# Hybrid encoder block on one core: moving the matmul operands to byte addresses that are multiples of 256 or 2048

## The chip, the cores and the metric

The kernel runs on one core of a Trainium2 chip. The metric is the device time of one execution in microseconds (us); lower is better.

## The reference

One layer of a hybrid sequence encoder, batch 1, 512 tokens, width 1024, all in float32. Cut to what matters here:

```
h = rms_norm(x, norm1_g)
p = h @ w_in                                  # 1024 -> 11520 columns: the "projections"
y_a = b_a * causal_dwconv(c_a * x_a)          # short gated convolution
y_b = rg_lru(causal_dwconv(x_b)) * gelu(g_b)  # linear recurrence over the tokens
y_c = rwkv7(token_shift(p_c)) * g_c           # matrix-state recurrence, 16 heads, chunks of 64
m = gate_a*y_a + gate_b*y_b + gate_c*y_c
x = x + m @ w_out                             # 1024 -> 1024
x = x + square(relu(rms_norm(x) @ mlp_w1)) @ mlp_w2   # 1024 -> 4096 -> 1024
return rms_norm(x, final_g)
```

## The kernel before

**Dense products.** Every dense float32 product is made of three matmuls. Each operand is split into a high part (the value rounded to the matmul's input type) and a low part (what is left), and `mm3` (lines 155 to 158) issues high times high, high times low, low times high, all into one PSUM tile. In each of them one operand is stationary (loaded into the array first, 128 x 128) and the other is streamed through it (128 x 512, or 128 x 256 where half the tokens are done).

**Weights.** `load_w` fetches 128 rows of weights in two halves of 128 x 512. `load_half` (lines 130 to 137) issues the DMA from the SP queue into `raw`, ScalarE casts it to the high part `whi` (L134), and VectorE subtracts to get the low part `wlo` (the helper `tt`, L97). There are three buffers for `raw` and four each for `whi` and `wlo`; all lie next to each other in the memory of each partition. 340 halves go through these buffers in all.

**Stages**, in order of time (us from the start of the span):

- 0 to 30: the tokens' norm; weights begin to load.
- 30 to 747: projections. 90 chunks of 128 output columns. For 87 of them `proj` (from L271) streams the normed input `hh`, `hl` (eight slices of 512 tokens each) against the weights, so the weight is stationary: 24 matmuls a chunk, into PSUM tile `pp`. Three first chunks use the unscaled input `xgh`, `xgl` instead. Between them stand the small matmuls of the recurrence (`pA`, `pu`, `py`, `pS`, ...) and small dense products (`pga`, `pgi` with the weights `swbh`, `swbl` and the streamed operand `uh`, `ul`).
- 747 to 770: `w_out`, eight chunks for each half of the tokens, 24 matmuls of 256 columns each, streaming `mh`, `ml`; PSUM tile `acc`. (The first half's matmuls lie partly before 747.)
- 770 to 953: first MLP product, 32 chunks (`fi`), streaming `h2h`, `h2l` against weights; PSUM tile `p1`, which the profile calls `p`. The first chunk is done in two halves of 256 columns. ScalarE and VectorE make the squared ReLU of each chunk and its parts `ah`, `al` (`ah2`, `al2` from chunk 24 on).
- 953 to 1130: second MLP product. Here the roles are swapped: slices of `ah`, `al` are stationary, and the weights `whi`, `wlo` are streamed, into eight PSUM tiles `acc`; 32 x 24 matmuls.
- 1130 to 1137: the last norm and the output.

**What sets the order.** The kernel is written in a tile language. Its scheduler fixes one order of instructions for each engine, from the order of the code and the priorities in it (`OFF`, `CP`, `R0` and others). Places in memory come from pools: a tile of a pool that grows from the left follows the tile before it, one of a pool on the right (`htp`, `pro`, `wk`, `h2p`, `xrp`) is counted down from the end of the partition. No address is written by hand; the default alignment is 32 bytes.

Of the kernel before, what the change touches and what calls it, by code (L numbers as in the profile page):

```python
# [10 lines left out]
F32R = mybir.dt.float32r  # L11
# [7 lines left out]
P = 128  # L19
# [8 lines left out]
NWARM = 2  # L28
POOL_KT = (1, 3, 5, 6, 7)
S = 512  # L30
D = 1024
KT = 8
NG = 4
# [3 lines left out]
NF = FF // P  # L37
# [54 lines left out]
def block_kernel(ctx, tc, xt, win, par, mulr, sw, wout, w1, w2, fg, cst, eyes, out):  # L92
# [18 lines left out]
    wp = ctx.enter_context(tc.tile_pool(name="wp", bufs=2))  # L111
# [18 lines left out]
    def load_half(src, i):  # L130
        raw = wp.tile([P, S], F32, tag="raw", name="raw", bufs=3)
        sy.dma_start(raw, src[:, i * S:(i + 1) * S])
        hi = wp.tile([P, S], F32R, tag="whi", name="whi", bufs=4)
        ac.copy(hi, raw)  # L134
        lo = wp.tile([P, S], F32R, tag="wlo", name="wlo", bufs=4)
        tt(lo, raw, f(hi), SUB)
        return hi, lo

# [8 lines left out]
    def split(pool, src, tag, rows=slice(0, P), bufs=None):  # L147
        th, tl = tag if type(tag) is tuple else (tag + "h", tag + "l")
        hi = pool.tile([P, S], F32R, tag=th, name=th, bufs=bufs)
        lo = pool.tile([P, S], F32R, tag=tl, name=tl, bufs=bufs)  # L150
        ac.copy(hi[rows], src)
# [36 lines left out]

    ht_ctx = ExitStack()
    htp = ht_ctx.enter_context(tc.tile_pool(name="htp", bufs=1, side="right"))  # L190
    hh = htp.tile([P, KT, S], F32R, name="hh")
    hl = htp.tile([P, KT, S], F32R, name="hl")

    ps = ExitStack()
    pp = ps.enter_context(tc.tile_pool(name="pp", bufs=3, space=PSUM))
# [3 lines left out]
    pro = pro_ctx.enter_context(tc.tile_pool(name="pro", bufs=1, side="right"))  # L199
# [2 lines left out]
    xT = sp.tile([P, KT, S], F32, tag="AXt", name="xT")  # L202
    xgh_ = [sp.tile([P, 4, S], F32R, tag=t, name="xgh") for t in ("BKT", "Z")]
    xgh = lambda kt: xgh_[kt // 4][:, kt % 4]
    xgl = pro.tile([P, KT, S], F32R, name="xgl")
    rsb = pro.tile([P, S], F32, name="rsb")
    ones = pro.tile([P, P], F32, name="ones")
    zer = sp.tile([P, S], F32, tag="dg", name="zer")
# [439 lines left out]
    M = {"done": []}  # L648
# [152 lines left out]
    def open_m():  # L801
        pk_ctx.close()
        mo = mo_ctx.enter_context(tc.tile_pool(name="mo", bufs=1))
        mh = M["mh"] = mo.tile([P, KT, S], F32R, name="mh")
        ml = M["ml"] = mo.tile([P, KT, S], F32R, name="ml")
        mab = M["mab"] = mo.tile([P, 2, S], F32, name="mab")
        for q in M["done"]:
            gp.dma_start(mh[:, q], mhd[q])
            gp.dma_start(ml[:, q], mld[q])
        gp.dma_start(mab, mpd[6:8].rearrange("q p t -> p q t"))  # L810
        M["mo"] = mo
        return
        yield

    def last_fill():
        yield from fill_main(NG - 1)
        M["gts"] = []
        for h in range(2):
            q = 6 + h
            gt = yield from gate_c(sp, q, f"bv{h}")  # L820
            g2_mul(wk, q, gt)
            M["gts"].append(gt)
            yield
        wk_ctx.close()
        ht_ctx.close()
        h2p = h2_ctx.enter_context(tc.tile_pool(name="h2p", bufs=1, side="right"))
        M["h2h"] = h2p.tile([P, KT, S], F32R, name="h2h")
        M["h2l"] = h2p.tile([P, KT, S], F32R, name="h2l")
        xrp = xr_ctx.enter_context(tc.tile_pool(name="xrp", bufs=1, side="right"))
        M["xrp"] = xrp  # L830
        x2T = M["x2T"] = xrp.tile([P, KT, S], F32, name="x2T")
        for i in range(4):
            gp.dma_start(x2T[:, 2 * i:2 * i + 2], xt[2 * i:2 * i + 2].rearrange("k p t -> p k t"))
        while "half" not in M:
            yield
        fin_m(0)
        yield from w_out(0)
# [53 lines left out]
    h2h, h2l = M["h2h"], M["h2l"]  # L891
# [6 lines left out]
    NA = 3 * NF // 4  # L898
    with tc.tile_pool(name="mw", bufs=2) as mw, \
            tc.tile_pool(name="ap", bufs=1) as apool, \  # L900
            ExitStack() as apool2:
        ahs = [apool.tile([P, NA, S], F32R, name="ah")]
        als = [apool.tile([P, NA, S], F32R, name="al")]
        ahl = lambda fi: (ahs[fi // NA][:, fi % NA], als[fi // NA][:, fi % NA])

        def mlp1(t, w, tl):
            for kt in range(KT):
                wh, wl = wslice(w, kt)
                mm3(t[:, tl], wh, wl, h2h[:, kt, tl], h2l[:, kt, tl],
                    start=kt == 0, stop=kt == KT - 1)  # L910

        for fi in range(NF):
            t = pp.tile([P, S], F32, tag="pp", name="p1")
            w = load_w(w1[fi])
            if fi == 0:
                for th in range(2):
                    mlp1(t, w, slice(th * HT, (th + 1) * HT))
            else:
                mlp1(t, w, slice(0, S))
            if fi == 0:  # L920
                drain(to_tokens(1))
            r = mw.tile([P, S], F32, tag="r", name="r")
            ac.activation(r, t, AF.Relu)
            tt(r, r, r, MUL)
            if fi == NA:
                xr_ctx.close()
                ap2 = apool2.enter_context(tc.tile_pool(name="ap2", bufs=1))
                ahs.append(ap2.tile([P, NF - NA, S], F32R, name="ah2"))
                als.append(ap2.tile([P, NF - NA, S], F32R, name="al2"))
            ahi, alo = ahl(fi)  # L930
            ac.copy(ahi, r)
            tt(alo, r, f(ahi), SUB)
        ac.activation(epst, epst, AF.Sqrt)
        gp.memset(epst, EPS)

        sc2 = cp.tile([P, 4], F32, name="sc2")
        tt(sc2, ss2[:, 0], ss2[:, 1], ADD)
        ts2(sc2, sc2, 1.0 / D, EPS, MUL, ADD)
        v.reciprocal(sc2, sc2)
        h2_ctx.close()  # L940
        with tc.tile_pool(name="fin", bufs=1, side="right") as fin:
            xr = fin.tile([P, 4, D], F32, name="xr2")
            gp.dma_start(xr, x2d.rearrange("i p d -> p i d"))
            fgt = fin.tile([P, D], F32, name="fgt")
            gp.dma_start(fgt, fg.to_broadcast([P, D]))
            bank = lambda pool, tag: pool.tile([P, S], F32, tag=tag, name="acc")
            acc = [[bank(pc, "pu"), bank(pc, "pS")], [bank(pc, "py"), bank(pm, "pm")],
                   [bank(pm, "pm"), bank(pp, "pp")], [bank(pp, "pp"), bank(pp, "pp")]]

            def mlp2(fi, w, i, h):  # L950
                ms = slice(i * P, (i + 1) * P)
                ahi, alo = ahl(fi)
                mm3(acc[i][h], ahi[:, ms], alo[:, ms], w[h][0], w[h][1],
                    start=fi == 0, stop=fi == NF - 1)

            for fi in range(NF - 2):
                w = load_w(w2[fi])
                for i in range(4):
                    for h in range(2):
                        mlp2(fi, w, i, h)  # L960
            wl2 = [load_w(w2[fi]) for fi in range(NF - 2, NF)]
            def last(i):
                ss = fin.tile([P, 2], F32, tag="fss", name="fss", bufs=2)
                x3f = xr[:, i] if i < 3 else fin.tile([P, D], F32, name="x3f")
                for h in range(2):
                    hs = slice(h * S, (h + 1) * S)
                    for d_ in range(2):
                        mlp2(NF - 2 + d_, wl2[d_], i, h)
                    stt(xr[:, i, hs], acc[i][h], sc2[:, i:i + 1], xr[:, i, hs], MUL, ADD)
                    junk = fin.tile([P, S], F32, tag="fj", name="fj", bufs=2)  # L970
                    ac.activation(junk, xr[:, i, hs], AF.Square, accum_out=ss[:, h:h + 1])
                    (v if (i, h) == (3, 0) else gp).tensor_tensor(out=x3f[:, hs], in0=xr[:, i, hs], in1=fgt[:, hs], op=MUL)
                sd = fin.tile([P, 2], F32, tag="fsd", name="fsd", bufs=2)
                tt(sd[:, 0:1], ss[:, 0:1], ss[:, 1:2], ADD)
                ac.activation(sd[:, 1:2], sd[:, 0:1], AF.Sqrt, bias=epst[:, 0:1], scale=1.0 / D)
                v.reciprocal(sd[:, 0:1], sd[:, 1:2])
                yield
                for h in range(2):
                    hs = slice(h * S, (h + 1) * S)
                    if h == 0 and i != 2:  # L980
                        ac.activation(x3f[:, hs], x3f[:, hs], AF.Copy, scale=sd[:, 0:1])
                    else:
                        v.tensor_scalar(out=x3f[:, hs], in0=x3f[:, hs], scalar1=sd[:, 0:1], scalar2=None, op0=MUL)
                    (ac if h == 0 and i != 2 else sy).dma_start(out[i, :, hs], x3f[:, hs])

            gens = [last(i) for i in range(4)]
            for i in (0, 1, 2, 0, 1, 3, 3, 2):
                next(gens[i], None)
        ps.close()
# [74 lines left out]
```

## Time and profile before

| What | Value |
|---|---|
| median of three executions | 1141.97 us (1141.84 to 1142.87) |
| the profiled execution's own time | 1139.16 us |
| its span, first to last instruction | 1137.4 us |
| mean granted TensorE clock | 0.985 of full speed |
| TensorE matmuls (PE) busy | 1102.8 us, 97% of the span |
| VectorE (DVE) busy | 786.2 us, 69% |
| ScalarE (ACT) busy | 549.1 us, 48% |
| mean DMA rate | 101 GB/s |

How to read it: matmuls overlap. One of 512 columns is shown as some 0.39 to 0.41 us long, but the next one starts after some 0.23 us, so the distance from start to start is what a matmul costs in a dense row of them, not its duration.

### The profile page before, as it was taken

How to read it: one execution, taken by the hardware profiler on the slowest of the kernel's cores; microseconds unless marked ns; L12 is line 12 of the kernel's file. 1: busy time of each engine (PE TensorE's matmuls, PEld its weight loads, DVE VectorE, ACT ScalarE, POOL GpSimd, SP SyncE). 2: the span in 40 equal slices, each digit the busy share in tenths (PEclk: the TensorE clock that was granted, in tenths of full speed). 3: DMA queues.
4: the chain of work that ended last, by engine and by line, in shares of the span. 5: the costliest groups of instructions: out<-in, count | busy, mean ns of one | idle time of the engine just before them, and what ended most of it. 6: DMA issues, size and time to landing. Idle time of an engine off the chain costs nothing.

```text
span 1137.4 us, 17256 instructions
## 1 busy us (share of the span) xinstructions
PE 1102.8 (97%) x6396; PEld 867.8 (76%) x6396; DVE 786.2 (69%) x1537; ACT 549.1 (48%) x1005; POOL 58.9 (5%) x99
## 2 busy tenths in 40 slices
PE   8899989999999999999999999999999999999996
PEld 4677877778777778777777667898888888888885
DVE  7998996889976979976979957786444444222225
ACT  6655456534557534557534565565444443222224
POOL 3200000000000000000000020100000000000003
PEclk8899999999999999999999999999999999999998
DMA  5222222222332222332221262554322225322232
GB/s 190 76 95 63 85 83 71 71 93 68 95 112 76 76 93 68 101 107 75 75 89 65 84 195 75 176 188 160 96 94 94 93 93 178 107 95 93 93 102 93
DMA packets 61973, 114.69 MB, mean 101 GB/s; under 512 B 7232, under 2 KB 10816, under 8 KB 61888
## 3 DMA queue, kind: packets, MB, share of 16 engines
q1 hardware_dynamic: 54960, 95.49, 26.0%
q0 software_dynamic: 6352, 17.30, 4.7%
q8 instruction: 50, 0.82, 0.3%
q10 hardware_dynamic: 576, 0.79, 0.2%
q14 instruction: 35, 0.29, 0.1%
HBM read 104.64 MB, written 8.91 MB: 100 GB/s over the span
## 4 chain that ended last, share of the span: by engine, by line
PE 81%; DVE 14%; issue 3%; ACT 2%; DMA 0%; SPq 0%; DVEq 0%; ACTq 0%
PE pp L158 11%; PE pp L156 11%; PE pp L157 11%; PE acc L157 6%; PE acc L156 6%; PE acc L158 6%; PE p L158 5%; PE p L156 5%; PE p L157 5%; DVE wlo L97 3%; PE pA L461 2%; DVE Z L97 2%; DVE dg L97 2%; PE py L568 1%; DVE g L100 1%
## 5 line engine op out<-in xcount | busy, mean ns | idle before, releaser
L97 DVE TENSOR_TENSOR wlo<-raw,whi 128x512 fp32r<-128x512 f32 x340 | 235.8, 696 | 242.0 <-ACT whi L134 232.3
L134 ACT CAST whi<-raw 128x512 fp32r<-128x512 f32 x340 | 209.8, 619 | 364.3 <-PE acc L158 122.7
L158 PE MATMUL pp<-hh,wlo 128*128 128x512 f32 x696 | 284.0, 409 | 14.8 <-DVE wlo L97 14.7
L157 PE MATMUL pp<-hl,whi 128*128 128x512 f32 x696 | 281.5, 404 | 3.1 <-DVE hl L100 3.1
L156 PE MATMUL pp<-hh,whi 128*128 128x512 f32 x696 | 281.9, 406 | 1.3 <-ACT hh L257 1.3
L158 PEld LDWEIGHTS pp<-hh,wlo 128*128 128x128 f32 x696 | 132.6, 191 | 52.7 <-DVE wlo L97 21.7
L157 PEld LDWEIGHTS pp<-hl,whi 128*128 128x128 f32 x696 | 132.5, 190 | 34.1 <-DVE hl L100 3.7
L156 PEld LDWEIGHTS pp<-hh,whi 128*128 128x128 f32 x696 | 132.6, 190 | 32.8 <-ACT hh L257 1.8
L158 PE MATMUL p<-h2h,wlo 128*128 128x512 f32 (+1 forms) x264 | 103.0, 390 | 0.0
L156 PE MATMUL p<-h2h,whi 128*128 128x512 f32 (+1 forms) x264 | 102.9, 390 | 0.0
L157 PE MATMUL p<-h2l,whi 128*128 128x512 f32 (+1 forms) x264 | 102.8, 389 | 0.0
L157 PE MATMUL acc<-wlo,ah 128*128 128x512 f32 x256 | 99.7, 389 | 0.0
L156 PE MATMUL acc<-whi,ah 128*128 128x512 f32 x256 | 99.6, 389 | 0.0
L158 PE MATMUL acc<-whi,al 128*128 128x512 f32 x256 | 99.6, 389 | 0.0
L158 PEld LDWEIGHTS p<-h2h,wlo 128*128 128x128 f32 x264 | 49.7, 188 | 11.4
L157 PEld LDWEIGHTS p<-h2l,whi 128*128 128x128 f32 x264 | 49.7, 188 | 11.3
L156 PEld LDWEIGHTS p<-h2h,whi 128*128 128x128 f32 x264 | 49.7, 188 | 11.2
L157 PEld LDWEIGHTS acc<-wlo,ah 128*128 128x128 f32 x256 | 48.0, 188 | 10.1 <-DVE wlo L97 0.3
L156 PEld LDWEIGHTS acc<-whi,ah 128*128 128x128 f32 x256 | 48.0, 188 | 10.1
L158 PEld LDWEIGHTS acc<-whi,al 128*128 128x128 f32 x256 | 48.1, 188 | 10.0
L97 DVE TENSOR_TENSOR dg<-Z 64x31 f32<-64x31 f32 (+15 forms) x124 | 42.2, 340 | 4.1
L97 DVE TENSOR_TENSOR Z<-Z,dg 64x31 f32<-64x31 f32 (+15 forms) x124 | 42.2, 340 | 4.1
(299 smaller groups left out, 1525.4 us busy)
## 6 DMA issues: line engine op xcount, KB each, us to landing
raw<-in_win SPq DMA_DIRECT2D x180, 256.0 KB, 2.6
raw<-in_w SPq DMA_DIRECT2D x128, 256.0 KB, 2.6
raw<-in_wout SPq DMA_DIRECT2D x32, 256.0 KB, 2.6
swr<-in_sw SPq DMA_DIRECT2D x16, 128.0 KB, 2.2
x2T<-in_xt POOLq DMA_DIRECT2D x4, 512.0 KB, 6.3
x2d<-st POOLq DMA_DIRECT2D x8, 256.0 KB, 3.2
xr<-x2d POOLq DMA_DIRECT2D x1, 2048.0 KB, 8.9
xT<-in_xt SPq DMA_DIRECT2D x3, 512.0 KB, 6.1
```

The source lines that it names most:

```text
L97: return v.tensor_tensor(out=o, in0=a, in1=b, op=op)
L100: return v.scalar_tensor_tensor(out=o, in0=a, scalar=s, in1=b, op0=op0, op1=op1)
L134: ac.copy(hi, raw)
L156: pe.matmul(ps, wh, xh, start=start, stop=False)
L157: pe.matmul(ps, wh, xl, start=False, stop=False)
L158: pe.matmul(ps, wl, xh, start=False, stop=stop)
L461: pe.matmul(pts[h][:, ci], G_.BK[rows, jj, c], G_.AR[rows, jj, c], start=True, stop=True)
L568: mm = pe.matmul(py[64 * h:64 * h + 64, jj], w, x, start=first and jj == 0, stop=last, skip_group_check=True)
```

## The change

Tiles that are operands of the dense matmuls get an alignment: `AL` = 256 bytes, and `ALM` = 2048 bytes for the streamed operand of the first MLP product and the stationary one of the second.

```
+AL, ALM = 256, 2048
     def load_half(src, i):
-        hi = wp.tile([P, S], F32R, tag="whi", name="whi", bufs=4)
+        hi = wp.tile([P, S], F32R, tag="whi", name="whi", bufs=4, align_bytes=AL)
-        lo = wp.tile([P, S], F32R, tag="wlo", name="wlo", bufs=4)
+        lo = wp.tile([P, S], F32R, tag="wlo", name="wlo", bufs=4, align_bytes=AL)
...
+    hh = htp.tile([P, KT, S], F32R, name="hh", align_bytes=AL)
+    hl = htp.tile([P, KT, S], F32R, name="hl", align_bytes=AL)
...
+    xgl = pro.tile([P, KT, S], F32R, name="xgl", align_bytes=AL)
...
+        mh = M["mh"] = mo.tile([P, KT, S], F32R, name="mh", align_bytes=AL)
+        ml = M["ml"] = mo.tile([P, KT, S], F32R, name="ml", align_bytes=AL)
...
+        M["h2h"] = h2p.tile([P, KT, S], F32R, name="h2h", align_bytes=ALM)
+        M["h2l"] = h2p.tile([P, KT, S], F32R, name="h2l", align_bytes=ALM)
...
+        ahs = [apool.tile([P, NA, S], F32R, name="ah", align_bytes=ALM)]
+        als = [apool.tile([P, NA, S], F32R, name="al", align_bytes=ALM)]
...
+                ahs.append(ap2.tile([P, NF - NA, S], F32R, name="ah2", align_bytes=AL))
+                als.append(ap2.tile([P, NF - NA, S], F32R, name="al2", align_bytes=AL))
```

The two built programs hold the same 9,856 instructions, in the same order on each engine and with the same waits. What differs is where tiles lie in each partition. The table gives the byte address of each operand as built, and its remainder by 256 and by 512. All buffers of a tag lie 2048 bytes apart and the 512-byte slices of weights that a matmul loads follow each other, so every stationary slice of `whi` has the remainder of the table too; the same holds for all slices of the others (a half of the tokens is 1024 bytes).

| Tile | before: address, by 256, by 512 | after: address, by 256, by 512 |
|---|---|---|
| `whi` (first buffer) | 25152, 64, 64 | 25344, 0, 256 |
| `wlo` (first buffer) | 33344, 64, 64 | 33792, 0, 0 |
| `hh`, `hl` | 196576 and 212960, 224, 480 | 196352 and 212736, 0, 256 |
| `xgh` | 59968, 64, 64 | 60416, 0, 0 |
| `xgl` | 170720, 224, 224 | 170240, 0, 256 |
| `mh` | 123072, 192, 192 | 123648, 0, 256 |
| `ml` | 139456, 192, 192 | 140288, 0, 0 |
| `h2h`, `h2l` | 196576 and 212960, 224, 480 | 194560 and 210944, 0, 0 |
| `ah`, `al` | 47680 and 96832, 64, 64 | 49152 and 100352, 0, 0 |
| `ah2` | 145984, 64, 64 | 150528, 0, 0 |
| `al2` | 162368, 64, 64 | 167168, 0, 256 |
| `uh`, `ul`, `swbh`, `swbl` (no alignment asked) | 175072, 177120, 185312, 186336: 224, 480 | 174624, 176672, 184864, 185888: 32, 32 |

The other tiles of the recurrence move by a few hundred bytes with their pools.

More of the change, by code (lines that the diff above doesn't have):

```diff
@@ L190, in block_kernel @@
     htp = ht_ctx.enter_context(tc.tile_pool(name="htp", bufs=1, side="right"))
-    hh = htp.tile([P, KT, S], F32R, name="hh")
-    hl = htp.tile([P, KT, S], F32R, name="hl")
+    hh = htp.tile([P, KT, S], F32R, name="hh", align_bytes=AL)
+    hl = htp.tile([P, KT, S], F32R, name="hl", align_bytes=AL)
     ps = ExitStack()
@@ L204, in block_kernel @@
     xgh = lambda kt: xgh_[kt // 4][:, kt % 4]
-    xgl = pro.tile([P, KT, S], F32R, name="xgl")
+    xgl = pro.tile([P, KT, S], F32R, name="xgl", align_bytes=AL)
     rsb = pro.tile([P, S], F32, name="rsb")
@@ L803, in open_m @@
         mo = mo_ctx.enter_context(tc.tile_pool(name="mo", bufs=1))
-        mh = M["mh"] = mo.tile([P, KT, S], F32R, name="mh")
-        ml = M["ml"] = mo.tile([P, KT, S], F32R, name="ml")
+        mh = M["mh"] = mo.tile([P, KT, S], F32R, name="mh", align_bytes=AL)
+        ml = M["ml"] = mo.tile([P, KT, S], F32R, name="ml", align_bytes=AL)
         mab = M["mab"] = mo.tile([P, 2, S], F32, name="mab")
@@ L826, in last_fill @@
         h2p = h2_ctx.enter_context(tc.tile_pool(name="h2p", bufs=1, side="right"))
-        M["h2h"] = h2p.tile([P, KT, S], F32R, name="h2h")
-        M["h2l"] = h2p.tile([P, KT, S], F32R, name="h2l")
+        M["h2h"] = h2p.tile([P, KT, S], F32R, name="h2h", align_bytes=ALM)
+        M["h2l"] = h2p.tile([P, KT, S], F32R, name="h2l", align_bytes=ALM)
         xrp = xr_ctx.enter_context(tc.tile_pool(name="xrp", bufs=1, side="right"))
@@ L901, in block_kernel @@
             ExitStack() as apool2:
-        ahs = [apool.tile([P, NA, S], F32R, name="ah")]
-        als = [apool.tile([P, NA, S], F32R, name="al")]
+        ahs = [apool.tile([P, NA, S], F32R, name="ah", align_bytes=ALM)]
+        als = [apool.tile([P, NA, S], F32R, name="al", align_bytes=ALM)]
         ahl = lambda fi: (ahs[fi // NA][:, fi % NA], als[fi // NA][:, fi % NA])
@@ L927, in block_kernel @@
                 ap2 = apool2.enter_context(tc.tile_pool(name="ap2", bufs=1))
-                ahs.append(ap2.tile([P, NF - NA, S], F32R, name="ah2"))
-                als.append(ap2.tile([P, NF - NA, S], F32R, name="al2"))
+                ahs.append(ap2.tile([P, NF - NA, S], F32R, name="ah2", align_bytes=AL))
+                als.append(ap2.tile([P, NF - NA, S], F32R, name="al2", align_bytes=AL))
             ahi, alo = ahl(fi)
```

## The prediction

> **What bounds the kernel now.** First the page's busy times and its chain of work that ended last:
>
> ```profile
> PE 1102.8 (97%) x6396; PEld 867.8 (76%) x6396; DVE 786.2 (69%) x1537; ACT 549.1 (48%) x1005; POOL 58.9 (5%) x99
> ...
> PE 81%; DVE 14%; issue 3%; ACT 2%; DMA 0%; SPq 0%; DVEq 0%; ACTq 0%
> PE pp L158 11%; PE pp L156 11%; PE pp L157 11%; PE acc L157 6%; PE acc L156 6%; PE acc L158 6%; PE p L158 5%; PE p L156 5%; PE p L157 5%; DVE wlo L97 3%; PE pA L461 2%; DVE Z L97 2%; DVE dg L97 2%; PE py L568 1%; DVE g L100 1%
> ```
>
> TensorE sets the end: 81% of the chain, of which `pp` (projections) 33%, `acc` (mostly the second MLP product) 18% and `p` (the first) 15%. So I ask what one matmul costs. A window inside the projections, one of the first MLP product and one of the second:
>
> ```profile
> 200.00:300.00 100.00, 99.86 (x585) 76.93 (x585) 88.13 (x183) 49.88 (x92) 2.79 (x6) 1.00 0.24 77
> 758.00:768.00 10.00, 10.00 (x87) 10.00 (x86) 8.08 (x16) 6.50 (x14) 0.54 (x1) 1.00 0.60 204
> 800.00:940.00 140.00, 140.00 (x599) 112.54 (x598) 66.48 (x100) 59.00 (x100) 0.00 (x0) 1.00 0.29 94
> 955.00:1035.00 80.00, 80.00 (x355) 66.24 (x354) 20.38 (x30) 18.47 (x30) 0.48 (x1) 1.00 0.38 129
> ```
>
> Columns: window, then busy us and count of PE, weight loads, DVE, ACT, POOL, then granted clock, DMA share, GB/s. In both MLP windows PE never idles and the granted clock is 1.00, the matmuls have the same shape, and yet the first makes 599 in 140 us (234 ns each) and the second 355 in 80 us (225 ns each). A count includes one or two begun before its window, so the exact distance comes from the start times (first column):
>
> ```profile
> 945.05 0.39 PE L156 MATMUL p<-h2h,whi 128*128 128x512 f32 x1
> 945.28 0.40 PE L157 MATMUL p<-h2l,whi 128*128 128x512 f32 x1
> 945.51 0.40 PE L158 MATMUL p<-h2h,wlo 128*128 128x512 f32 x1
> ...
> 948.33 0.39 PE L158 MATMUL p<-h2h,wlo 128*128 128x512 f32 x1
> ```
>
> From 945.05 to 948.33 there are 14 steps: 234.3 ns each. The second product:
>
> ```profile
> 954.84 0.39 PE L156 MATMUL acc<-whi,ah 128*128 128x512 f32 x1
> 955.07 0.39 PE L157 MATMUL acc<-wlo,ah 128*128 128x512 f32 x1
> 955.29 0.39 PE L158 MATMUL acc<-whi,al 128*128 128x512 f32 x1
> ...
> 957.56 0.39 PE L156 MATMUL acc<-whi,ah 128*128 128x512 f32 x1
> ```
>
> Twelve steps in 2.72 us: 226.7 ns. So two rates exist, 7.6 ns apart, at one clock and one shape. What differs is where the operands lie. In the table of addresses, the streamed `h2h` has remainder 224 by 256 and the stationary `whi` 64: unequal. In the second product both sides have 64: equal. A third place tells whether the value or the equality matters:
>
> ```profile
> 92.18 0.40 PE L156 MATMUL pp<-hh,whi 128*128 128x512 f32 x1
> 92.41 0.40 PE L157 MATMUL pp<-hl,whi 128*128 128x512 f32 x1
> ...
> 93.57 0.39 PE L156 MATMUL pgi<-uh,swbh 128*128 128x512 f32 x1
> ...
> 94.25 0.40 PE L156 MATMUL pp<-hh,whi 128*128 128x512 f32 x1
> ```
>
> The three `pgi` matmuls, from 93.57 to 94.25, take 226.7 ns each amid the projections, with DVE and ACT at work. Their operands `uh`, `ul`, `swbh`, `swbl` all have remainder 224: equal again, though not 64. The `pp` row before (224 against 64) takes 230 ns in this piece. So I read: equal remainders give 226.7, unequal ones 234.3. It is a regularity in rows, not a mechanism that they show.
>
> **The change part by part.** It puts `whi`, `wlo` and every dense partner at remainder 0 by 256, so unequal pairs become equal. No instruction, DMA or wait is added, removed or moved; the order on each queue is the same. Only durations can change.
>
> *First MLP product.* 31 chunks x 24 = 744 matmuls, 7.6 ns each: 5.7 us. All of it lands, since PE has no idle time there and DVE is busy 66.48 of 140 us, ACT 59.00: there is room.
>
> *Projections.* 87 chunks x 24 = 2088 matmuls x 7.6 = 15.9 us at most. Not all of it lands:
>
> ```profile
> L158 PE MATMUL pp<-hh,wlo 128*128 128x512 f32 x694 | 282.7, 408 | 14.8 <-DVE wlo L97 14.7
> L156 PE MATMUL pp<-hh,whi 128*128 128x512 f32 x693 | 280.2, 406 | 0.0
> L157 PE MATMUL pp<-hl,whi 128*128 128x512 f32 x694 | 280.1, 404 | 0.0
> L97 DVE TENSOR_TENSOR wlo<-raw,whi 128x512 fp32r<-128x512 f32 x190 | 130.2, 687 | 42.2 <-ACT whi L134 36.9 <-PE pu L561 2.3 <-issue 0.2
> L97 DVE TENSOR_TENSOR ul<-u,uh 128x512 fp32r<-128x512 f32 x8 | 5.5, 692 | 0.5
> ```
>
> (After the bar: busy us, mean ns, then idle time before and what ended it.) The chain holds 33% of 1137.4 us in `pp`, 375 us, or 1,600 matmuls at 234.3: 12.2 us of the 15.9. The rest runs beside DVE's stretches of the chain, which do not shrink. And PE already waits 14.7 us for `wlo`, with DVE at 88.13 of 100 us, so a PE 3% faster will catch up with it more often. I take 10 us. Low end 5 (DVE takes over half the chain), high end 15.9.
>
> *`w_out`.* 8 x 2 x 24 = 384 matmuls of 256 columns, `mh` at 192 against 64: unequal. From the window 758 to 768 with 87 of them, less two begun earlier, one takes 118 ns; half of the equal rate is 113.3. Their difference over 384 is 1.8 us, some of which falls into bubbles: 1.5. Bounds 0 and 1.8.
>
> *Second MLP product.* 768 matmuls, equal before and after: 0. No row has remainder 0 on a dense pair, so this is the unknown. Its faster bound comes from the start, where the clock is granted at half:
>
> ```profile
> 34.00:38.00 4.00, 4.00 (x11) 0.50 0.02 4
> ...
> 33.80 0.63 PE L158 MATMUL pp<-hh,wlo 128*128 128x512 f32 x1
> ...
> 36.37 0.63 PE L156 MATMUL pp<-xgh,whi 128*128 128x512 f32 x1
> ```
>
> Six steps in 2.57 us are 428 ns, so 214 at full clock if nothing else held it up. Its slower bound is the longest single step between the rows of the first product:
>
> ```profile
> 946.21 0.40 PE L158 MATMUL p<-h2h,wlo 128*128 128x512 f32 x1
> 946.45 0.40 PE L156 MATMUL p<-h2h,whi 128*128 128x512 f32 x1
> ```
>
> that is 240 ns in rounded times. I take 226.7, because `pgi` and the second product reach the same value at remainders 224 and 64: it does not depend on which remainder it is.
>
> *Splitting on ACT and DVE.* The same subtraction takes 687 ns for `wlo` (remainder 64) and 692 for `ul` (224): VectorE does not notice, so 0. *The recurrence's small matmuls*: their tiles shift together with their pools, so I count 0; if they moved, the 2% of the chain in `pA` is the largest piece.
>
> *Alignment to 2048 instead of 256.* The four slices of `ah` stand 0, 512, 1024 and 1536 bytes off the streamed tile by 2048, and all run at 226.7. I cost this part at nothing.
>
> *Sum:* 5.7 + 10 + 1.5 = 17.2 us. Against the profiled execution's 1139.2 that is 1122.0; the median of three is 2.8 us above it, so the forecast is 1142.0 - 17.2 = **1124.8 us**.
>
> **Against two rules.** The rows give a price for unequal places. The Trainium skill speaks against one: "SBUF — State Buffer", section "Who interferes with whom", gives TensorE two read ports, one for the streamed operand and one for weight loads, and says that PE and ACT never wait on anyone. By that rule this change would be worth nothing; the 234.3 against 226.7 ns at one clock does not agree with it. "TensorE: Matmul & The Clock Gate", section "Back-to-back issue gap", gives N / 2.4 + 2.5 ns for an isolated pair, which would be an estimate of 216 ns for 512 columns, with no term for an address; no row at full clock is that short on average, and by it the sum would again be zero.
>
> **The rivals.**
>
> *Equal by 256 is not enough; it must be equal by 512.* All equal pairs above are equal by 512 too (64 and 64, 480 and 480), so the rows cannot tell. After the change `whi` has 256 by 512 and `wlo` 0. Then of each three matmuls, the projections get two right (hh 256), the first MLP product one, `w_out` one, and the second MLP product loses two of three in its first 24 chunks and one of three in the last 8. That is 10 x 2/3 + 5.7/3 + 1.5/3 = 9.1 gained, and 576 x 2/3 x 7.6 ns + 192/3 x 7.6 ns = 3.4 lost: 5.7 us, 1136.3. For it: nothing excludes it. Against: nothing but that a multiple of 256 is the smaller period.
>
> *Remainder 0 is better still.* Every dense matmul goes towards the 214 of the bound. Half way there, 6.3 ns more on 1,512 MLP matmuls and on the 10/12.2 of 1,600 that land, is 17.8 us: 1107. Against it: 64 and 224 give the same 226.7.
>
> *Nothing happens.* The two rates come from something else that differs between the stages: the second product puts three matmuls into a PSUM tile and goes on to the next, as `pga` and `pgi` do, while the projections put 24 into one. Then 1142.0. Against it: within a group of three the step is no longer than between groups (954.84, 955.07, 955.29).
>
> *Slower.* Two reads that start at the same remainder 0 meet at the same place of the memory all the time, and the second MLP product, now the fastest, rises to the 240 of the longest step: 768 x 13.3 ns = 10.2 us lost, and the first product and the projections, at 240 too, lose 5.7 ns on 744 and some 1,300: 11.6 more. 1163.8. It decides for slower from 229.7 ns in the second product on, if nothing else gains. Against it: its pairs meet at equal remainders already.
>
> **How the numbers follow.** Forecast 0.55 (its own range 1118 to 1132, from the ends of the projections' term), equal by 512 0.15 (1136), better still 0.12 (1107), nothing 0.10 (1142), slower 0.08. What a measurement of this kernel can tell from no change is about 0.2%, 2.3 us. The first three are faster: 0.82; same 0.10; slower 0.08. A range from 1112 to 1143 leaves out the slower case and the better one, 0.20.
>
> **What would show it.** In the changed profile: starts in the first MLP product 226.7 ns apart without the swing between 230 and 240; windows 140 us long with 617 matmuls in place of 599; the second product still at 226.7; the idle time before L158 in the projections above 14.8 us, by some 2 us and `<-DVE wlo`. The forecast is wrong if the second MLP product changes, if L156 and L158 come to differ in step (the rule by 512), or if `pp` gets faster and the span does not.

## The result and the profile after

The changed kernel takes 1132.5 us (median of four executions, 1130.94 to 1133.29), the kernel before 1142.42 in the same comparison (1141.84 to 1144.3). The ratio is 0.9917, with a 95% interval of 0.9894 to 0.994: 9.9 us or 0.8% faster. The forecast was 1124.8 us, 17.2 us faster. The profiled execution of the changed kernel took 1130.94 us (span 1129.1), against 1139.16 (1137.4) before: 8.2 us apart. The distances by stage below are between these two.

First the page's busy times and its chain of work that ended last. Line numbers are two higher than before, so L158 to L160 are the three matmuls of `mm3`, L99 the subtraction and L136 the cast.

```profile
PE 1090.0 (97%) x6396; PEld 866.7 (77%) x6396; DVE 786.8 (70%) x1537; ACT 549.2 (49%) x1005; POOL 59.6 (5%) x99
...
PE 82%; DVE 13%; issue 3%; ACT 2%; DMA 0%; SPq 0%; DVEq 0%; ACTq 0%
```

PE has lost 12.8 us of busy time, and the other engines do the same work as before. Next the windows (busy us and count of PE, weight loads, DVE, ACT, POOL, then clock, DMA share, GB/s): inside the projections, the first MLP product, the second.

```profile
200.00:300.00 100.00, 99.34 (x599) 77.16 (x596) 88.55 (x185) 50.88 (x95) 2.91 (x7) 1.00 0.23 75
...
800.00:940.00 140.00, 140.00 (x619) 115.95 (x618) 68.69 (x103) 60.53 (x103) 0.00 (x0) 1.00 0.29 97
955.00:1035.00 80.00, 80.00 (x354) 66.25 (x353) 20.62 (x30) 18.67 (x30) 0.00 (x0) 1.00 0.31 103
```

The first product makes 619 matmuls in the 140 us that held 599, and the second makes 354 where it made 355. The start times of single matmuls give the step:

```profile
935.73 0.39 PE L158 MATMUL p<-h2h,whi 128*128 128x512 f32 x1
935.96 0.39 PE L159 MATMUL p<-h2l,whi 128*128 128x512 f32 x1
936.18 0.39 PE L160 MATMUL p<-h2h,wlo 128*128 128x512 f32 x1
...
945.25 0.39 PE L158 MATMUL acc<-whi,ah 128*128 128x512 f32 x1
...
948.20 0.39 PE L159 MATMUL acc<-wlo,ah 128*128 128x512 f32 x1
```

From 935.73 to 945.25 lie 42 steps of the first product, 226.7 ns each, and then 13 of the second, 226.9 by these rounded times. Both products now run at one rate, without the swing up to 240.

In the projections the picture is mixed. The groups by line, with the idle time before them last:

```profile
L160 PE MATMUL pp<-hh,wlo 128*128 128x512 f32 x696 | 280.8, 404 | 18.5 <-DVE wlo L99 18.4
L159 PE MATMUL pp<-hl,whi 128*128 128x512 f32 x696 | 277.8, 399 | 3.1 <-DVE hl L102 3.1
```

and the waits, of the kernel before and then of the changed one (us in total, times, longest):

```profile
PE pp L158 <- DVE wlo L97: 14.7, 11, 3.4
```

```profile
PE pp L160 <- DVE wlo L99: 18.4, 18, 4.0
```

The matmuls are shorter, and PE waits for `wlo` 18 times instead of 11, for 3.7 us more.

When each stage starts (us from the start of the span) tells where the 8.2 us came from:

| Milestone | before | after | gained so far |
|---|---|---|---|
| first `pu` of line 561 (563 after), first quarter of the projections | 181.92 | 181.98 | -0.1 |
| last quarter, first `pA` | 588.75 | 587.75 | 1.0 |
| first matmul of `w_out` | 712.09 | 709.01 | 3.1 |
| first MLP product | 771.55 | 768.83 | 2.7 |
| second MLP product | 953.48 | 945.25 | 8.2 |
| one of its last matmuls | 1127.03 | 1118.80 | 8.2 |

The first MLP product gave 5.5 us, the projections 3.1, the stretch of `w_out` took 0.4 back, and the second product stayed as it was.

These are two single executions, and the granted clock differs between them: from 155 to 190 us its mean was 0.90 before and 0.80 after, from 650 to 665 us 0.89 and 1.00. By an estimate from these rows (0.10 of 35 us, less 0.11 of 15 us) the clock cost the changed kernel's projections some 2 us here, most of it in the first row of the table. By the medians, which are 9.9 us apart, the projections and `w_out` together gained 4.4 us rather than 2.7.

### The profile page after: what moved, and what is told of

It is laid out like the page before. It is cut to its first block, busy times and chain, and to the rows that moved or that the text cites. A ratio compares the mean times of both kernels' runs of the same rounds, so it can differ in the third digit from the quotient of the medians.

```text
span 1129.1 us, 17256 instructions
## 1 busy us (share of the span) xinstructions
PE 1090.0 (97%) x6396; PEld 866.7 (77%) x6396; DVE 786.8 (70%) x1537; ACT 549.2 (49%) x1005; POOL 59.6 (5%) x99
## 4 chain that ended last, share of the span: by engine, by line
PE 82%; DVE 13%; issue 3%; ACT 2%; DMA 0%; SPq 0%; DVEq 0%; ACTq 0%
PE pp L160 12%; PE pp L158 12%; PE pp L159 11%; PE acc L159 6%; PE acc L158 6%; PE acc L160 6%; PE p L160 5%; PE p L159 5%; PE p L158 5%; DVE wlo L99 3%; PE pA L463 2%; DVE Z L99 2%; DVE dg L99 2%; PE py L570 1%; PE pu L555 1%
## 5 line engine op out<-in xcount | busy, mean ns | idle before, releaser
L99 DVE TENSOR_TENSOR wlo<-raw,whi 128x512 fp32r<-128x512 f32 x340 | 235.7, 696 | 231.4 <-ACT whi L136 222.7
L136 ACT CAST whi<-raw 128x512 fp32r<-128x512 f32 x340 | 209.6, 619 | 353.4 <-PE acc L160 123.1
L160 PE MATMUL pp<-hh,wlo 128*128 128x512 f32 x696 | 280.8, 404 | 18.5 <-DVE wlo L99 18.4
L159 PE MATMUL pp<-hl,whi 128*128 128x512 f32 x696 | 277.8, 399 | 3.1 <-DVE hl L102 3.1
L158 PE MATMUL pp<-hh,whi 128*128 128x512 f32 x696 | 278.5, 402 | 1.6 <-ACT hh L259 1.5
L160 PEld LDWEIGHTS pp<-hh,wlo 128*128 128x128 f32 x696 | 132.1, 190 | 55.4 <-DVE wlo L99 27.9
L158 PEld LDWEIGHTS pp<-hh,whi 128*128 128x128 f32 x696 | 132.2, 190 | 29.9 <-ACT hh L259 1.9
L160 PE MATMUL p<-h2h,wlo 128*128 128x512 f32 (+1 forms) x264 | 101.2, 383 | 0.0
L158 PE MATMUL p<-h2h,whi 128*128 128x512 f32 (+1 forms) x264 | 101.2, 383 | 0.0
L158 PE MATMUL acc<-whi,ah 128*128 128x512 f32 x256 | 99.6, 389 | 0.0
L160 PE MATMUL acc<-whi,al 128*128 128x512 f32 x256 | 99.6, 389 | 0.0
L158 PEld LDWEIGHTS p<-h2h,whi 128*128 128x128 f32 x264 | 49.6, 188 | 9.6
L160 PEld LDWEIGHTS p<-h2h,wlo 128*128 128x128 f32 x264 | 49.6, 188 | 9.5
L158 PEld LDWEIGHTS acc<-whi,ah 128*128 128x128 f32 x256 | 48.0, 188 | 10.1
L160 PEld LDWEIGHTS acc<-whi,al 128*128 128x128 f32 x256 | 48.0, 188 | 10.0
L99 DVE TENSOR_TENSOR Z<-Z,dg 64x31 f32<-64x31 f32 (+15 forms) x124 | 42.2, 340 | 4.1
L99 DVE TENSOR_TENSOR dg<-Z 64x31 f32<-64x31 f32 (+15 forms) x124 | 42.2, 340 | 4.1
```

Source lines behind the costliest of these rows:

```text
L99: return v.tensor_tensor(out=o, in0=a, in1=b, op=op)
L158: pe.matmul(ps, wh, xh, start=start, stop=False)
L159: pe.matmul(ps, wh, xl, start=False, stop=False)
L160: pe.matmul(ps, wl, xh, start=False, stop=stop)
```

## The experiments

**One part alone: only the MLP operands and the weights.** The changed kernel, with the alignment taken off the operands of the projections and of `w_out`:

```
-    hh = htp.tile([P, KT, S], F32R, name="hh", align_bytes=AL)
+    hh = htp.tile([P, KT, S], F32R, name="hh")
     # the same for hl, xgl, mh, ml
```

> The changed kernel with the projections' and the output product's streamed operands put back: hh, hl again at remainder 224 by 256, mh, ml at 128, weights whi, wlo and the MLP operands as changed. Theory 1 (the price of a matmul hangs on whether the streamed and the stationary operand have the same remainder by 256): first MLP product at 226.7 ns a step, projections back at 234 ns, so the first product alone gains 5.6 us and the projections' share of 2.7 to 3 us is lost again: about 1136.5 us against 1142.4 before and 1132.5 changed. Rival (the projections' share is only scatter between runs): 1133 to 1134, the same as the changed kernel.

Measured: 1137.09 us (1135.02 to 1139.17, nine runs) against 1141.72 (twelve runs); ratio 0.9964, interval 0.9947 to 0.9981. The first MLP product takes 5.6 us less than before. The projections are back: the product starts at 773.32, 1.8 us later than before the change, and the steps of `pp` up to 260 ns, now with operands 224 bytes apart, are 233.2 ns on average. So the two gains are separate, and each belongs to the pairs of operands that were made equal.

**Equal, but neither a multiple of 256 nor equal by 512.** The kernel before, with 160 bytes of filling behind `hl` and behind `h2l`. These pools are counted down from the end, so `hh`, `hl`, `h2h` and `h2l` move from remainder 224 to 64 by 256, where `whi` and `wlo` already stand. By 512 they are 320 against 64, still unequal.

```
     hl = htp.tile([P, KT, S], F32R, name="hl")
+    htp.tile([P, 40], F32, name="padh")
...
         M["h2l"] = h2p.tile([P, KT, S], F32R, name="h2l")
+        h2p.tile([P, 40], F32, name="padh2")
```

> The kernel before, no tile aligned; a pad of 160 bytes behind hl and another behind h2l moves hh, hl, h2h, h2l from remainder 224 to 64 by 256, where whi and wlo lie already (320 against 64 by 512). Theory 1 (equal remainders count, not which): first MLP product and projections at 226.7 ns, second product unchanged, time as the changed kernel, 1132 to 1134 us. Rival (a multiple of 256, a start on a line of the memory, is what counts): 234.3 ns as before, 1142 us. Rival (equal by 512 is needed): first product still slow.

Measured: 1132.03 us (1129.56 to 1133.57); ratio 0.9929, interval 0.9904 to 0.9953. By the medians it is the whole gain of the change, from two unused tiles. (Its profiled execution was the slowest of the four, at a mean clock of 0.981; in it the first product starts at 771.18, only 0.4 us earlier than before, so the share of the projections can't be read from that one execution.) The window of the first product in this kernel:

```profile
800.00:940.00 140.00, 140.00 (x620) 115.91 (x619) 68.61 (x103) 61.01 (x104) 0.00 (x0) 1.00 0.29 98
```

620 matmuls in the 140 us: the full rate, at remainder 64. What counts is that both operands have the same remainder by 256; that it is 0 counts for nothing, and equality by 512 or 2048 isn't needed.

**Four distances.** The changed kernel with `h2h`, `h2l` begun r bytes behind an aligned place (the streamed side of the first product), and `ah`, `al` r' bytes behind one (the stationary side of the second, in its first 24 chunks). Four kernels, with r and r' of 32 and 32, 64 and 64, 128 and 128, 16 and 96. For 16 and 96:

```
+        M["h2h"] = h2p.tile([P, KT * S + 64], F32R, name="h2h", align_bytes=512)[:, 4:4 + KT * S].rearrange("p (k s) -> p k s", k=KT)
         # the same for h2l; ah and al with [:, 24:24 + NA * S]
```

> The changed kernel with h2h, h2l 32 bytes off a multiple of 512, and ah, al (first 24 chunks) 32 bytes off too, so that the streamed operand of the first MLP product and the stationary one of the second have remainder 32 against weights at 0. Any theory of equal remainders (by 64, 128 or 256): first product back at 234 ns a step (5.7 us lost), second product slow for the first time, some 234 ns in its first 576 matmuls (4.4 us lost) and 226.7 in the last 192. Rival (only the streamed operand's start matters): second product stays at 226.7.

> As the 32-byte run, with 64 bytes. Theory 1 as I put it (equal by 256): both products at about 234 ns. Rival (equal by 64 is enough): both at 226.7 ns, time as the changed kernel.

> As the 32-byte run, with 128 bytes. Equal by 256: both products at about 234 ns. Equal by 64 or by 128: both at 226.7 ns.

> As the 32-byte run, with 16 bytes for h2h, h2l and 96 for ah, al. Equal remainders by 32 or more: both slow. If the excess grows with the offset, 16 bytes gives a smaller one than the 32-byte run, and 96 a larger one; if it is a yes or no, both read 234 ns.

Measured, one execution each: 1139.3, 1139.34, 1139.24 and 1138.63 us. The one execution of the kernel before beside them took 1144.55 us. All four are slower than the changed kernel, in both products: the first takes 180.5 to 181.2 us with r of 16, 32 and 128, and 177.9 with 64 (176.4 in the changed kernel, 181.9 before), the second 177.3 to 178.4 us up to the start of its last matmul (174.0 in both). The mean distance from start to start in each product, without the few over 260 ns, by how far the streamed operand stands behind the stationary one by 256 bytes (the rows for 0 and 160 also hold the kernels before and after):

| Streamed minus stationary, by 256 | step, 512 columns | where |
|---|---|---|
| 0 | 226.7 ns | both products after; second product before (227.0 in the last 8 chunks of the second in all four) |
| 16 | 231.7 | first product, r = 16 |
| 32 | 233.3 | first product, r = 32 |
| 64 | 228.9 | first product, r = 64 |
| 128 | 233.3 and 232.4 | first product, r = 128; second, r' = 128 |
| 160 | 234.3 and 234.3 | first product before; second, r' = 96 |
| 192 | 233.3 | second product, r' = 64 |
| 224 | 233.3 | second product, r' = 32 |

The second product of the kernel with 16 and 96, which runs at 226.7 in the kernel before and after, has become the first product of before:

```profile
954.83 0.40 PE L158 MATMUL acc<-whi,ah 128*128 128x512 f32 x1
955.07 0.39 PE L159 MATMUL acc<-wlo,ah 128*128 128x512 f32 x1
955.30 0.40 PE L160 MATMUL acc<-whi,al 128*128 128x512 f32 x1
...
956.47 0.40 PE L159 MATMUL acc<-wlo,ah 128*128 128x512 f32 x1
```

Seven steps in 1.64 us, 234.3 ns each, and the single steps show the same pattern of seven (231 234 235 234 231 238 237 ns). There the two lay 160 apart as the tiles happened to fall; here the stationary one was moved to that distance. So the distance sets the step, whichever side is moved. Of the distances other than 0, 64 costs least: the theory as it was put, 234 ns there too, missed in the first product. The excess is smaller at 16 than at 32 and larger at 160, but because of 64 it doesn't simply grow with the distance. Why that is so, and why 128 reads a little differently in the two products, the runs don't tell. Nor do they tell whether the place of a matmul's own stationary operand counts or that of the next one's, whose load runs beside it.

**The projections with less work on VectorE.** The theory was that VectorE, 88 of 100 us busy there, gives back what PE gains. To test it, the loop of 31 steps in `inverse` (two VectorE operations a step, four times) was left out of the kernel before and of the changed one; these two don't compute the inverse, and the pair is compared with itself. Leaving it out also lets the scheduler order the rest differently, but the two of the pair have one order.

```
         for s in range(31):
-            tt(tv, la[:, s, s + 1:32]..., xt[:, 0:c, s:s + 1]..., MUL)
-            tt(xt[:, 0:c, s + 1:32], xt[:, 0:c, s + 1:32], tv, ADD)
```

> The kernel before without the 31 steps of the inverse's loop on VectorE (124 products and 124 sums left out, 84 us of VectorE work; the output is another). It serves as the base of the next run. Theory 2 (in the projections the gain is eaten by waits for wlo, because VectorE's queue is too full to deliver the weights sooner): 20 to 60 us faster than 1142, and idle time before wlo's matmul well under 14.7 us. Rival (order and latencies of the recurrence's chain limit the stage, not VectorE's load): idle time before wlo's matmul unchanged.

> The changed kernel without the same loop. Theory 2: with VectorE unloaded the projections keep most of their 13.5 us of shorter steps, so the distance to the run before this one grows from 9.9 us (before against changed) to 15 to 19 us: 5.6 in the first MLP product and 9 to 13 in the projections. Rival (chain latency or the granted clock takes it): the distance stays at 8 to 10 us.

Measured: 1132.58 us (1129.04 to 1132.94; ratio to the kernel before 0.9929, interval 0.9903 to 0.9954) and 1115.19 us (1114.17 to 1116.3; ratio 0.978, interval 0.9755 to 0.9805). The first is a miss: 86 us of VectorE's work less (700.0 busy, from 786.2) make the kernel only some 10 us faster, not 20 to 60; its other sign, that the waits for `wlo` shrink, came. More could hardly be won: PE had been busy for 97% of the span, so all its idle time was under 35 us. The distance between the two is what was asked, and it is 17.4 us, against 9.9 with the loop. In the two profiled executions, 16.4 us apart at mean clocks of 0.989 and 0.988, the first MLP product gives 5.4, as ever; the projections and `w_out` together give 11.0 (the product starts at 763.27 and 752.30), against 2.7. The waits for `wlo` are gone. The groups of the kernel before without the loop, then of the changed one:

```profile
L158 PE MATMUL pp<-hh,wlo 128*128 128x512 f32 x696 | 280.7, 404 | 0.0
```

```profile
L160 PE MATMUL pp<-hh,wlo 128*128 128x512 f32 x696 | 276.8, 398 | 0.1
```

Here a projection's shorter step is worth nearly all that it saves: the steps of `pp` up to 260 ns sum to 12.9 us less, and 11.0 arrive. What ate the gain is shown, then, as far as this pair goes: VectorE's load, together with the order that goes with it. The pair doesn't separate the two.

**Relieving VectorE without leaving work out.** If VectorE holds the projections back, two of its products (`cs = xs*cs` and `y = bs*y`, 16 operations) could go to GpSimd, which is 5% busy. Done on the changed kernel and on the one before; a third kernel also moves the sum `gb + yc`.

```
-        tt(cs, xs, cs, MUL)
+        gp.tensor_tensor(out=cs, in0=xs, in1=cs, op=MUL)
...
-        tt(y, bs, y, MUL)
+        gp.tensor_tensor(out=y, in0=bs, in1=y, op=MUL)
```

> The changed kernel with two products of each short-convolution chunk (cs = xs * cs and y = bs * y, 16 in all, 128x512) moved from VectorE to GpSimd, whose products of this size take 1.3 to 1.6 us in the trace. All results are computed. Theory 2 (VectorE's queue holds the projections back): VectorE is relieved of 16 x 0.69 = 11 us, part of it in the stages where it is the bound; 2 to 6 us faster than the changed kernel, 1127 to 1130. Rival (the longer operation and its hand-over delay the chunk, or GpSimd and VectorE hinder each other): no gain, or slower than 1132.5.

> The kernel before with the same two products moved to GpSimd. Theory 2: some gain, smaller than with the change, since TensorE at 234 ns a step waits less for VectorE: 1139 to 1142, and the distance to the run before this one grows from 9.9 to 11 to 14 us. Rival: the distance stays at 9 to 10.

> As the first run of this group, with a third operation (gb = gb + yc, six of them) moved to GpSimd too. Theory 2: another 4 us of VectorE relieved, 0 to 2 us faster than the first. Rival: GpSimd's queue, which also issues the loads of yc and the stores of the merged parts, delays them, so it is slower than the first.

Measured, beside 1142.65 us for the kernel before: 1141.39 (ratio 0.9998, interval 0.9979 to 1.0016), 1148.8 (1.005, 1.0026 to 1.0074) and 1142.82 (1.0011, 0.9995 to 1.0027). The theory's forecast missed in all three: the changed kernel loses its whole gain, as the first rival had it, and the distance between the first two is 7.4 us, under both expectations. So the runs don't confirm the theory; nor do they test whether less work on VectorE helps, since VectorE's busy time didn't fall: 791.3 us, from 786.8 in the changed kernel. Its waits for `wlo` hardly shrink (17.1 us, from 18.4), and new costs come. GpSimd takes 1530 and 1436 ns for a product, where VectorE's like operations take some 690, and ScalarE waits for it. The groups, then ScalarE's wait (us in total, times, longest):

```profile
L708 POOL TENSOR_TENSOR g<-g,g 128x512 f32<-128x512 f32 x8 | 12.2, 1530 | 182.6 <-ACT g L707 182.6
L717 POOL TENSOR_TENSOR g<-u,g 128x512 f32<-128x512 f32 x8 | 11.5, 1436 | 11.8 <-ACT whi L136 5.5 <-ACT u L716 4.3 <-issue 1.5
```

```profile
ACT g L710 <- POOL g L708: 10.3, 7, 2.3
```

And VectorE's own operations beside it stretch. In the changed kernel, then in that with GpSimd's products:

```profile
L102 DVE SCALAR_TENSOR_TENSOR u<-u,u 128x512 f32<-128x512 f32 x16 | 11.0, 690 | 5.5 <-ACT u L684 5.2
...
L102 DVE SCALAR_TENSOR_TENSOR g<-g,u 128x512 f32<-128x512 f32 x8 | 5.5, 688 | 0.1
```

```profile
L102 DVE SCALAR_TENSOR_TENSOR u<-u,u 128x512 f32<-128x512 f32 x16 | 13.4, 836 | 6.1 <-ACT u L684 5.2 <-ACT u L696 0.7
...
L102 DVE SCALAR_TENSOR_TENSOR g<-g,u 128x512 f32<-128x512 f32 x8 | 8.7, 1082 | 0.1
```

The means hide two kinds. Of the 16 operations `u<-u,u`, three took 1464 to 1473 ns, and of the eight `g<-g,u` two took 2256 and 2275; each of these five ran beside a GpSimd product. The others took 677 to 694 ns, none of them beside one.

The mean granted clock fell too, from 0.984 to 0.974 in the profiled executions. It isn't the whole loss: the execution of this kernel at a mean clock of 0.983 took 1138.54 us, those of the changed kernel at 0.982 took 1132.72 and 1133.29, so 5 to 6 us remain. How these divide between the handover and the stretched operations was not settled. The fastest version found stays the changed kernel (with the one that only adds filling beside it).

## Why the prediction was right in sign and too high in size

The measured 1132.5 us lies just above the forecast's own range (1118 to 1132; the ends of its terms give 1118.6 to 1131.3). The wider range, 1112 to 1143, holds it because it reaches over the rivals "equal by 512" and "nothing".

**What bounds the kernel, and the regularity in the rows: right.** Equal remainders gave 226.7 ns and unequal ones 229 to 234 in both MLP products, and in the projections the steps up to 260 ns went from 234.0 to 228.2 on average. That unequal ones cost one amount, 7.6 ns, was too simple: at a distance of 64 it is 2.2. The runs turned it from a regularity into a cause: moving either operand alone makes and unmakes it.

**First MLP product: 5.7 us expected, 5.5 measured.** 617 matmuls were expected in the window, 619 came.

**Projections: 10 us expected (5 to 15.9), some 3 measured.** This is the term of the sum that was mis-sized, and its low end as well. The step that failed is the one from the chain's share to a gain: 375 us of the chain in `pp` were taken as matmuls that all stay on the path when they get shorter. But a chain holds for its own execution. Where VectorE comes a little behind PE, a shorter matmul turns into a longer wait. The text named this, as "will catch up with it more often", and priced it too low. The distances between successive starts, from 39 us to the first MLP product, show it (count and sum):

| Distance | before | after | difference |
|---|---|---|---|
| `pp` to the next, up to 260 ns | 1796, 420.3 us (234.0 ns) | 1785, 407.3 (228.2 ns) | -13.1 |
| `pp`, over 420 ns, next reads `wlo` | 21, 23.4 | 26, 28.8 | +5.4 |
| `pp`, other over 420 ns | 27, 12.8 | 31, 15.1 | +2.3 |
| all others | 276.0 | 278.5 | +2.5 |

The sum is -2.9 us, in place of -13.1. Of the 13.1, 10.5 are the shorter steps (1,785 by 5.87 ns, unrounded), the rest is steps that moved to the rows below. The longer waits are no accident of one execution. The steps from `pp` to a matmul that reads `wlo` that are longer than 432 ns (which leaves out steps at half clock) number 13 and sum to 20.0 and 20.5 us in the two profiled executions with unequal operands in the projections (the kernel before and the first experiment). In the six with equal ones (the changed kernel, the filling, the four distances) they number 18 to 20 and sum to 25.3 to 26.3 us. The start of the first MLP product scatters more, with the clock: 771.55 and 773.32 us in the two, 768.06 to 771.92 in the six, 2.8 us apart on average. The gain stops where VectorE leads: in the window from 247 to 340 us, while `inverse` runs, DVE is busy 82.28 of 93 us in the changed kernel, and up to 588 us only 1.0 us is gained; the lower clock from 155 to 190 us has a part in that. The pair without that loop gives 11.0 us instead (with `w_out`), near the term as it was predicted.

**`w_out`: a gain of 1.5 us expected, a loss of 0.4 measured.** The step that failed is "half of the equal rate is 113.3". With 256 columns equal remainders are no faster. The starts before, and then after:

```profile
754.59 0.28 PE L157 MATMUL acc<-ml,whi 128*128 128x256 f32 x1
...
757.19 0.28 PE L158 MATMUL acc<-mh,wlo 128*128 128x256 f32 x1
```

```profile
754.31 0.28 PE L160 MATMUL acc<-mh,wlo 128*128 128x256 f32 x1
...
757.19 0.28 PE L160 MATMUL acc<-mh,wlo 128*128 128x256 f32 x1
```

22 steps of 118.2 ns in this piece became 24 of 120.0; over the stage the mean of the steps under 140 ns went from 118.7 to 119.6. The kernel with the filling leaves `mh` and `ml` unequal, and its steps stay at 118.6. At half clock a step of `pp` takes 426.7 ns (mean of 36 before and of 33 after, so the excess of unequal operands shows at full clock alone). Half of that is 213.3 ns for full clock, and half again 106.7 for 256 columns; 226.7 and 120.0 are both 13.3 ns over: with equal remainders, at these two widths, the excess is one amount for each matmul, not a share of its columns. Halving the step halved that too.

**Second MLP product: 0 expected, 0.0 measured**, and the same for the alignment to 2048: nothing.

**The rivals.** "Equal by 512" fell: after the change the second product has pairs 0 against 256 by 512 and keeps 226.7, and the kernel with the filling is unequal by 512 in the projections and the first product and fast. The time alone would have misled here, since 1132.5 lies nearer to that rival's 1136.3 than to 1124.8; the steps decide it. "Remainder 0 is better still" and "slower" fell by the same 226.7. "Nothing happens" fell with the first product. The warning "`pp` gets faster and the span does not" came true for most of the projections' part.

**Against the two rules.** That TensorE's two reads cost each other nothing, as the Trainium skill has it ("SBUF — State Buffer", section "SBUF: two separate sides", where PE is said never to wait on anyone), doesn't agree with these runs: the same instructions take 226.7 or 234.3 ns by where the operands lie. That the two reads hinder each other is the nearest reading of it, and not shown. Its formula for an isolated matmul ("TensorE: Matmul & The Clock Gate", "Back-to-back issue gap", N / 2.4 + 2.5 ns) gives an estimate of 215.8 ns for 512 columns and 109.2 for 256. The steps with equal remainders are 10.9 and 10.8 ns above it: the form, columns by the clock plus a fixed amount, agrees, the amount in this kernel doesn't.

## What to carry to other kernels

Where matmuls follow each other without a gap, compare the start-to-start distance of stages with the same shape; if they differ at one granted clock, look at the byte addresses of the streamed and the stationary operand and make them equal by 256 bytes, by alignment or by a filling. This is shown here for 512 streamed columns; with 256 it did not help. Size the gain only where PE is alone on the path: here, where VectorE was 88% busy and PE already waited for it, most of what the shorter matmuls saved came back, above all as waits, and the waits in the trace of before didn't bound it. When a time lies between two theories, let a signature in the trace decide, not the nearer number.

## What was not expected of the hardware

- The step of a 512-column matmul depends on the distance of its two operands by 256 bytes: 226.7 ns at 0, 228.9 at 64, 231.7 at 16 and 232.4 to 234.3 at 32, 128, 160, 192 and 224.
- With 256 columns the sign turns: 119.6 ns on average at distance 0 (most steps are 120), 118.7 at 128 (`w_out`), 117.4 at 160 (the first chunk of the first MLP product, before) and 117.9 at 32 and 64 (the same chunk, in two of the kernels with distances).
- At half clock the distance makes no difference: 426.7 ns for 512 columns, before and after.
- VectorE operations with two inputs of 128 x 512, some 690 ns long, took 1464 to 1473 ns (three) and 2256 and 2275 ns (two) when a GpSimd product ran beside them.
